# Measured matmul steps, concurrent row halves and one shared port in the model that orders a streaming trunk's matmuls

## The chip, the cores and the metric

The kernel runs on one NeuronCore of one Trainium2 chip. The metric is device time in microseconds of one execution; the median of several runs is compared. Time before: 3200.01 us median of 3 runs (3194.38 to 3201.84).

## The reference

One mixer layer over 2048 tokens of width 1024, all in float32. The input is normalised and modulated, projected by one matrix, and split over three branches (latent attention, a chunked gMLP, RWKV-7); each branch is gated, projected, weighted by a sigmoid gate and summed; the sum is projected again, normalised and added to the input.

```python
shift, scale, gate = jnp.split(c_act @ w_ada[l] + b_ada[l], 3, axis=-1)
h = rmsnorm(x, pre_g[l]) * (1 + scale[:, None]) + shift[:, None]
q_lat, kv_lat, k_rope, gm_in, rw_in, z, g_logit = split_last(h @ w_in[l], IN_SPLITS)
y_mla = mla_mixer(q_lat, kv_lat, k_rope, ...)      # block-causal softmax attention, 8 heads
y_gm = gmlp_mixer(gm_in, ...)                      # u * (W_s v + b) in blocks of 128
y_rw, v_first = rwkv7_mixer(rw_in, ...)            # delta-rule state, 8 heads of 64
branches = jnp.stack([y_mla, y_gm, y_rw], axis=2) * silu(z)
proj = jnp.einsum('bsnw,nwd->bsnd', branches, w_br[l])
merged = jnp.sum(proj * jax.nn.sigmoid(g_logit), axis=2)
y = merged @ w_out[l]
x = x + gate[:, None] * rmsnorm(y, post_g[l])
```

## The kernel before

The tokens go in four super-blocks of 512 (s = 0 to 3). For each, a stage `wkv(s)` computes RWKV-7 and a stage `attention(s)` the latent attention. The large projections (`gemm`) are split products: activations and weights are each a high and a low float32r part, and `mm3` makes three matmuls of 512 columns for every 128 rows (`hh`, `hl` are the activations' parts, `wh`, `wl` the weights', `brh`, `brl` a branch's parts, `pd` the PSUM tile). A `gemm` over the width of 1024 is 24 such matmuls, one over half of it 12. ScalarE makes `wh`, and GpSimd or VectorE, whichever has the shorter backlog in the model, makes `wl` (`split`). The small steps of RWKV-7 and the transposes are plain float32.

TensorE takes its instructions in the order in which the program is written, and that order is made by a planner, the class `Pace`. Every piece of work is a generator (a thread) that yields what its next matmuls need: tiles, or a free PSUM tile of a ring (`RD`, `RS`, `RT`, `RO`: two of `pd`, three of `pss`, two of `pst`, one of `pso`). `Pace.run` keeps a rough clock of all engines. Of the threads whose needs are met by that clock, the first in rank goes on: rank 0 and 1 are the stage's own chains, 3 the projections of the next super-block (`todo`), 4 the gates and merges that only fill (`later`). Where no chain is ready, a filler runs until one is. So the clock decides how many `gemm` matmuls stand between two steps of a chain.

`Pace.note` advances that clock. It gives every instruction a duration, and `Pace.slot` finds the first free time of its engine. A result counts for another engine `HOP` = 0.25 us after its end. Weights are placed up to `EAR` = 8 us early (`pace.early`), and `gemm` then forgets them (`pace.forget`), so that no thread waits for them in the model. The lines that the change meets:

```python
if eng == "PE":
    dur = n * (4 if f32 and not i.is_transpose else 2 if f32 else 1) / 2400
    t = self.t = max(self.t, dep) + dur
...
    dur = .05 + n * .00084 + .04 * (not psum) + ...      # ScalarE
...
t = self.slot(eng, max(dep, self.t - self.early), dur) + dur
```

The chains that are spoken of below, all in `wkv`, once for each head pair `hp` of 0 to 3. `prepare`: two products per PSUM tile (`pst<-ard,bk`), ScalarE copies `abc`, VectorE masks `ak` and `MB`, then `m_ak_v` (`pso<-vt,ak`); ahead of it `v` is transposed into a `pst` tile that VectorE must first have read for `kk`. `inverses`: 31 steps on `X` through `tx`, all on VectorE and all in SBUF. `advance`: `pss<-Pm,xtb`, `pss<-u,m`, `pss<-n,xtb`, `pss<-MB,Wm` (64 rows, in the upper and the lower half of the array by turns), `pss<-UV,MB`. `states`: eight times `pss<-S,QG` with VectorE between them, then a normalisation over VectorE, ScalarE and GpSimd, and the transposes `pss<-consts,Y`. From s = 1 on, the output rows of the super-block before are finished in the same stage (`back`: `pst<-consts,yo`). A helper records every operation, so all of them have line 121.

Of the kernel before, what the change touches and what calls it, by code (L numbers as in the profile page):

```python
# [21 lines left out]
P = 128  # L22
# [69 lines left out]
class Pace:  # L92
    """Order of the tensor engine's work. Threads are generators that yield what their next piece of it needs:
    tiles (the last write to them), names of rings (a free tile), conditions. A rough clock of all engines says
    when a need should be met; of the threads whose need is met, the first in rank goes on."""
# [3 lines left out]
    def __init__(self):  # L99
        self.t = 0.0  # L100
        self.early = 0.0
        self.wrote, self.used = {}, {}
        self.busy = {}
        self.rings = {}
        self.lock = None
        self.cur = None
        self.threads = []
        self.pe = 0.0
        self.spent = 0.0
        self.table = None  # L110
        self.slots = {}

# [18 lines left out]
    def slot(self, eng, t, dur):  # L131
        """first time from t on at which the engine is free for dur"""
        b = self.busy.setdefault(eng, [])
        while b and b[0][1] < self.t - 60:
            b.pop(0)
        for n, (s, e) in enumerate(b):
            if t + dur <= s:
                b.insert(n, (t, t + dur))
                return t
            t = max(t, e)  # L140
        b.append((t, t + dur))
        return t
# [5 lines left out]
    def note(self, i):  # L148
        eng = str(i.engine).split(".")[-1]
        dma = "DMA" in type(i).__name__  # L150
        src, dst, n, full, f32 = [], [], 1, 0, False
        for l, aps in ((src, i.ins), (dst, i.outs)):
            for a in aps:
# [10 lines left out]
                if eng != "PE" or l is dst:  # L164
                    n = max(n, m)
# [8 lines left out]
        if eng == "PE":  # L174
            dur = n * (4 if f32 and not i.is_transpose else 2 if f32 else 1) / 2400
            t = self.t = max(self.t, dep) + dur
            self.pe += dur
# [5 lines left out]
        else:  # L183
            psum = any(x.startswith(("pd", "ps")) for x in src)
            op = type(i).__name__
            if eng == "Activation":
# [4 lines left out]
                dur = .05 + n * .00084 + .04 * (not psum) + .09 * (len(src) > 1) + .09 * (len(dst) > 1)  # L191
# [11 lines left out]
            t = self.slot(eng, max(dep, self.t - self.early), dur) + dur  # L203
# [10 lines left out]
    def forget(self, *tiles):  # L214
        """no wait for the last write to them"""
# [3 lines left out]
    def pool(self, pl, bufs):  # L219
        """its tiles wait for the last use of the tile that had their place"""  # L220
# [48 lines left out]
    def run(self, until, share=0.0, spare=lambda: True):  # L269
        """until the condition holds; per time of the threads of rank 0 and 1, share of those of rank 3;  # L270
        while nothing is to spare, the threads of rank 4 run only where the others wait for long"""
# [33 lines left out]
def trunk(ctx, tc, io, out):  # L305
# [38 lines left out]
    # ---------------------------------------------------------------- constants  # L344
# [13 lines left out]
    def rstd_of(dst, src, mul, eps, n):  # L358
        """dst = (src * mul + eps) ** -0.5"""
# [24 lines left out]
    with ExitStack() as st:  # L384
# [3 lines left out]
        # c -> silu(c) as columns  # L388
# [29 lines left out]
        # halves of the biases that go inside tanh(x / 2), and of k_a  # L418
# [6 lines left out]
        # x of the first super-block, normalised and transposed  # L425
# [58 lines left out]
    def output_gate(pl):  # L484
        """gate of the modulation times post_g, for all partitions"""
# [21 lines left out]
    # ---------------------------------------------------------------- shared pieces  # L507
# [24 lines left out]
    def split(hi, lo, src, e=None):  # L532
        """hi + lo == src, both float32r"""
# [6 lines left out]
    def wgran(src):  # L540
        """a [512, 128] piece of a weight matrix: [128 rows, 4, 128] high and low"""
# [13 lines left out]
    def gemm(w, c0, rhs, nk=KD, r0=0):  # L555
        """features c0..c0+127 of rhs' tokens, features on the partitions"""
# [16 lines left out]
    def silu2(n, f):  # L573
        """2 * silu(z) of branch n, features f"""
# [7 lines left out]
    def br_split(b2, pl=brp):  # L582
        """half of b2 as high and low"""
# [9 lines left out]
    def front_units(s, pl):  # L593
        """normalised, modulated input of a super-block, transposed, as high and low"""
# [72 lines left out]
    # ---------------------------------------------------------------- latent attention: projections  # L667
# [14 lines left out]
    def trig_of(s, pl):  # L682
        """rows 64..95: cosine, rows 96..127: signed sine"""
# [18 lines left out]
    def rope(dst, src, trig, t1, t2):  # L702
        """src rows 64..95 hold the halves, rows 96..127 the halves exchanged"""
# [4 lines left out]
    def mla_units(s, pl):  # L708
# [28 lines left out]
        def norms():  # L737
            """1 / rms of every token as a column, then as a row for all partitions"""
# [98 lines left out]
    # ---------------------------------------------------------------- gMLP  # L837
# [42 lines left out]
    def gm_gates(s):  # L880
        """the spatial gates times gelu(u) and 2 * silu(z)"""
# [17 lines left out]
    # ---------------------------------------------------------------- RWKV-7  # L899
    def latents():  # L900
        """of the decay and of the rate"""
# [14 lines left out]
    def wkv(s):  # L916
# [6 lines left out]
        with ExitStack() as st:  # L923
# [32 lines left out]
            def prepare(hp, r, k, v, sq, kk):  # L956
                pc = slice(hp * P, (hp + 1) * P)
                # decay, cumulated inside the chunks
# [18 lines left out]
                # squared norm of kk  # L977
# [18 lines left out]
                # b = kk * a / |kk|^2 with a = (1 + ta) / 2  # L996
# [13 lines left out]
                # tokens on the partitions  # L1010
# [13 lines left out]
                # products between the tokens of a chunk  # L1024
# [54 lines left out]
                # bonus  # L1079
# [10 lines left out]
            def inverses(hp, mb):  # L1090
                """of the 32 x 32 diagonal blocks; partition 32 g + x has rows g, g + 4, ... of block x's"""
# [21 lines left out]
            def advance(hp, xd, ard, el, Pm, vt, MB, abc):  # L1113
# [11 lines left out]
                # diagonal of the chunks' decays  # L1125
# [5 lines left out]
                # U = (I - M)^-1 [A | M_ak V]  # L1131
# [46 lines left out]
                # what a chunk adds by itself: output and state  # L1178
# [10 lines left out]
            def states(hp, zs, bv, QG, YH):  # L1189
                """chunk by chunk, then the normalised output"""  # L1190
# [18 lines left out]
                # normalisation over a head's channels  # L1209
# [64 lines left out]
    # ---------------------------------------------------------------- latent attention  # L1274
# [436 lines left out]
```

## Time and profile before

| | |
|---|---|
| time, median of 3 runs | 3200.01 us (3194.38 to 3201.84) |
| span of the profiled execution | 3209.0 us |
| TensorE busy | 3008.7 us, 94% |
| VectorE busy | 1943.6 us, 61% |
| ScalarE busy | 1473.8 us, 46% |
| GpSimd busy | 1186.6 us, 37% |
| mean granted clock of TensorE | 0.965 |

Read it so: TensorE (PE) is busy nearly all of the span, and its busy time counts a matmul until its modelled end, which overlaps the next one. VectorE (DVE) is busy 61%, ScalarE (ACT) 46%, GpSimd (POOL) 37% of the span. The granted clock is 1 where TensorE runs at 2.4 GHz and 0.5 where it runs at 1.2 GHz. The profiled execution's span lies 9 us over the median of the runs, and its own time is not listed apart from it.

### The profile page before, as it was taken

The page shows a single profiled execution, that of the slowest core. Times are in us where ns is not written, and L with a number is a line of the kernel's source. Part 1 is how long each engine was busy: PE and PEld are TensorE (multiplying, and loading weights), DVE is VectorE, ACT ScalarE, POOL GpSimd, SP SyncE. Part 2 cuts the span into 40 slices and gives each one's busy share as a digit, 9 for nine tenths or more (in the row PEclk, how much of TensorE's full clock was granted, in tenths as well). Part 3 has the DMA queues.
Part 4 walks back from the last instruction along what each step waited for, and adds up shares of the span by engine and source line. Part 5 has one row for each costly group of instructions (what it writes and reads, how often), then busy time and mean ns, then how long its engine had stood idle before and what let it go on. Part 6 is the DMA issues. An engine that isn't in the chain of part 4 may idle for free.

```text
span 3209.0 us, 47580 instructions
## 1 busy us (share of the span) xinstructions
PE 3008.7 (94%) x15900; PEld 2472.8 (77%) x15900; DVE 1943.6 (61%) x4800; ACT 1473.8 (46%) x3234; POOL 1186.6 (37%) x1114
## 2 busy tenths in 40 slices
PE   5899999989999999999999998999899999999998
PEld 4687777778777777878878776887787777788876
DVE  7436674474477765566367674557736766667653
ACT  4343332544433336555433434565444334477743
POOL 3333333343523334244443334224334333433324
PEclk8999999989999999999999998999999999999999
DMA  7443333745542466444544366444345425643345
GB/s 252 117 128 99 81 82 89 208 131 145 152 139 83 133 190 179 135 132 121 158 136 116 113 179 188 112 126 131 95 136 146 125 82 167 189 110 103 90 127 168
DMA packets 594113, 432.70 MB, mean 135 GB/s; under 512 B 143216, under 2 KB 489420, under 8 KB 593868
## 3 DMA queue, kind: packets, MB, share of 16 engines
q1 hardware_dynamic: 593696, 429.62, 47.0%
q8 instruction: 125, 2.05, 0.3%
q14 instruction: 120, 0.98, 0.1%
q10 hardware_dynamic: 172, 0.05, 0.0%
HBM read 328.61 MB, written 100.93 MB: 134 GB/s over the span
## 4 chain that ended last, share of the span: by engine, by line
PE 61%; DVE 21%; DMA 5%; issue 4%; ACT 2%; POOL 2%; SPq 1%; DVEq 0%; POOLq 0%; ACTq 0%
PE pd L121 37%; PE pst L121 11%; PE pss L121 9%; PE pso L121 5%; DVE X L121 4%; DVE tx L121 4%; DMA x<-in_x 2%; DVE y L121 1%; DVE QG L121 1%; DVE Y L121 1%; SPq L121 1%; DMA stg<-q_d 1%; DVE wl L121 1%; DVE gt L121 1%; DVE k L121 1%
## 5 line engine op out<-in xcount | busy, mean ns | idle before, releaser
L121 POOL TENSOR_TENSOR wl<-wr,wh 128x512 fp32r<-128x512 f32 x498 | 657.3, 1321 | 1111.3 <-ACT wh L121 1069.9
L121 PE MATMUL pd<-hh,wh 128*128 128x512 f32 x1952 | 810.8, 415 | 5.5 <-ACT hh L121 2.5
L121 PE MATMUL pd<-hl,wh 128*128 128x512 f32 x1952 | 771.3, 395 | 3.7 <-POOL hl L121 2.6
L121 PE MATMUL pd<-hh,wl 128*128 128x512 f32 x1952 | 771.8, 395 | 1.9 <-POOL wl L121 1.2
L121 ACT ACTIVATE wh<-wr 128x512 fp32r<-128x512 f32 x648 | 406.8, 629 | 796.9 <-PE pd L121 431.4
L121 PEld LDWEIGHTS pd<-hh,wl 128*128 128x128 f32 x1952 | 370.7, 190 | 85.6 <-DVE wl L121 1.8
L121 PEld LDWEIGHTS pd<-hh,wh 128*128 128x128 f32 x1952 | 372.0, 191 | 82.4 <-ACT wh L121 6.8
L121 PEld LDWEIGHTS pd<-hl,wh 128*128 128x128 f32 x1952 | 372.6, 191 | 68.9 <-POOL hl L121 3.6
L121 DVE TENSOR_TENSOR pw<-pst,ph 128x512 fp32r<-128x512 f32 (+2 forms) x352 | 196.3, 567 | 200.3 <-ACT ph L121 198.9
L121 PE MATMUL pd<-brh,wh 128*128 128x512 f32 x576 | 260.7, 453 | 30.9 <-DVE X L121 12.9
L121 ACT ACTIVATE ph<-pst 128x512 fp32r<-128x512 f32 (+2 forms) x352 | 171.9, 496 | 187.1 <-PE pst L121 155.0
L121 PE MATMUL pd<-brl,wh 128*128 128x512 f32 x576 | 239.3, 416 | 1.8 <-DVE brl L121 1.8
L121 PE MATMUL pd<-brh,wl 128*128 128x512 f32 x576 | 239.3, 415 | 0.0
L121 ACT ACTIVATE p<-p,nm 128x512 f32<-128x512 f32 (+3 forms) x288 | 189.5, 660 | 62.9 <-DVE nm L121 62.7
L121 DVE TENSOR_SCALAR_CACHE_REDUCE p<-pss 128x512 f32<-128x512 f32 (+2 forms) x320 | 192.2, 606 | 29.4 <-PE pss L121 25.5
L121 DVE TENSOR_TENSOR wl<-wr,wh 128x512 fp32r<-128x512 f32 x150 | 119.9, 801 | 85.3 <-ACT wh L121 77.9
L121 PE MATMUL pst<-consts,p 128*128 128x128 f32 x1088 | 162.7, 274 | 9.3 <-DVE otm L121 4.5
L121 PEld LDWEIGHTS pd<-brh,wh 128*128 128x128 f32 x576 | 116.4, 202 | 69.3 <-issue 24.3
L121 PE MATMUL pso<-ph,v 128*128 128x256 f32 x576 | 154.0, 289 | 2.3 <-ACT ph L121 2.3
L121 PE MATMUL pso<-pw,v 128*128 128x256 f32 x576 | 148.2, 285 | 4.0 <-DVE pw L121 2.3
L121 PEld LDWEIGHTS pst<-consts,p 128*128 128x128 f32 x1088 | 128.9, 141 | 27.6 <-DVE otm L121 5.0
L121 DVE TENSOR_TENSOR tx<-X,mb 128x60 f32<-128x60 f32 (+19 forms) x368 | 140.0, 380 | 8.7
(297 smaller groups left out, 5363.4 us busy)
## 6 DMA issues: line engine op xcount, KB each, us to landing
wr<-in_w_in SPq DMA_DIRECT2D x480, 256.0 KB
wr<-in_w_br SPq DMA_DIRECT2D x96, 256.0 KB
gate_d<-gt SPq DMA_DIRECT2D x64, 256.0 KB
part_d<-gt SPq DMA_DIRECT2D x64, 256.0 KB
p<-part_d SPq DMA_DIRECT2D x64, 256.0 KB
wr<-in_w_out SPq DMA_DIRECT2D x64, 256.0 KB
x<-in_x SPq DMA_DIRECT2D x56, 256.0 KB
gt<-gate_d SPq DMA_DIRECT2D x56, 256.0 KB
```

Of the source, the lines that this page charges most:

```text
L121: r = f(*a, **k)
```

## The change

Only the model's numbers and rules change; no operation of the computation does.

- TensorE, float32r: n / 2400 + 0.0135, at least 0.061 us, for n columns (512 columns: 0.227 for 0.213).
- TensorE, float32: twice max(0.111, n / 1200) (64 columns: 0.222 for 0.107; 128 columns: 0.222 for 0.213; 1 or 2 columns: 0.222 for about 0.002). Float32 transposes at least 0.108.
- A matmul on other rows of the array than the ones that began with it starts with them in the model, and adds only what it ends later (`beside`).
- ScalarE: 0.08 for 0.05 as the fixed part.
- GpSimd's instructions, and those of VectorE that read no PSUM, also occupy a common "port" in the model, so that they stand after each other.

```diff
+        self.beside = 0.0, [(0, P)]
...
-    def slot(self, eng, t, dur):
-        """first time from t on at which the engine is free for dur"""
-        b = self.busy.setdefault(eng, [])
-        while b and b[0][1] < self.t - 60:
-            b.pop(0)
-        for n, (s, e) in enumerate(b):
-            if t + dur <= s:
-                b.insert(n, (t, t + dur))
-                return t
-            t = max(t, e)
-        b.append((t, t + dur))
+    def slot(self, eng, t, dur, also=()):
+
+        lists = [self.busy.setdefault(e, []) for e in (eng, *also)]
+        for b in lists:
+            while b and b[0][1] < self.t - 60:
+                b.pop(0)
+        moved = True
+        while moved:
+            moved = False
+            for b in lists:
+                for s, e in b:
+                    if t < e and s < t + dur:
+                        t, moved = e, True
+        for b in lists:
+            insort(b, (t, t + dur))
         return t
...
         if eng == "PE":
-            dur = n * (4 if f32 and not i.is_transpose else 2 if f32 else 1) / 2400
-            t = self.t = max(self.t, dep) + dur
-            self.pe += dur
+            if f32 and not i.is_transpose:
+                dur = 2 * max(.111, n * 2 / 2400)
+            elif f32:
+                dur = max(.108, n * 2 / 2400)
+            else:
+                dur = max(.061, n / 2400 + .0135)
+            (r, c), (nr, nc) = i.tile_position, i.tile_size
+            if dep <= self.t and all(r >= b or r + nr <= a for a, b in self.beside[1]):
+
+                at = self.beside[0]
+                self.beside[1].append((r, r + nr))
+            else:
+                at = max(self.t, dep)
+                self.beside = at, [(r, r + nr)]
+            t, p = max(self.t, at + dur), self.t
+            self.pe += t - max(p, at)
+            self.t = t
...
-                dur = .05 + n * .00084 + .04 * (not psum) + .09 * (len(src) > 1) + .09 * (len(dst) > 1)
+                dur = .08 + n * .00084 + .04 * (not psum) + .09 * (len(src) > 1) + .09 * (len(dst) > 1)
...
-            t = self.slot(eng, max(dep, self.t - self.early), dur) + dur
+
+            port = ("port",) if eng == "Pool" or eng == "DVE" and not psum else ()
+            t = self.slot(eng, max(dep, self.t - self.early), dur, port) + dur
```

Every engine's order moves nearly throughout, and the number of matmuls stays (14001). The pattern of `wkv` repeats for s = 1, 2 and 3, before and after; the three places here are of s = 3. In the change the recording helper stands on line 123.

The first place is TensorE's order in `prepare` of head pair 1, from the products `ard`, `bk` to the first use of the masked `ak`. Before:

```order
8457 L121 MATMUL pst<-ard,bk 128x128 x8
8458 L121 MATMUL pd<-hh,wh 128x512
8459 L121 MATMUL pd<-hl,wh 128x512
8460 L121 MATMUL pd<-hh,wl 128x512
8461 L121 MATMUL pd<-hh,wh 128x512
8462 L121 MATMUL pd<-hl,wh 128x512
8463 L121 MATMUL pd<-hh,wl 128x512
8464 L121 MATMUL pd<-hh,wh 128x512
8465 L121 MATMUL pd<-hl,wh 128x512
8466 L121 MATMUL pd<-hh,wl 128x512
8467 L121 MATMUL pso<-vt,ak 128x64 x2
8468 L121 MATMUL pst<-ard,bk 128x128 x4
```

And the same step in the change:

```order
8502 L123 MATMUL pst<-ard,bk 128x128 x8
8503 L123 MATMUL pd<-hh,wh 128x512
8504 L123 MATMUL pd<-hl,wh 128x512
8505 L123 MATMUL pd<-hh,wl 128x512
8506 L123 MATMUL pso<-vt,ak 128x64 x2
8507 L123 MATMUL pst<-ard,bk 128x128 x4
8508 L123 MATMUL pd<-hh,wh 128x512
8509 L123 MATMUL pd<-hl,wh 128x512
8510 L123 MATMUL pd<-hh,wl 128x512
8511 L123 MATMUL pso<-vt,ak 128x64 x2
```

Three `gemm` matmuls stand ahead of the first `ak` step where nine stood, and three more stand ahead of the second, where there was none.

The second place is VectorE's queue ahead of that same `ak`: the last ten rows of it, which are the end of `inverses` of head pair 0 (`X`, `tx`) and one eviction of the merge (`gt`). Before:

```order
3159 L121 TENSOR_TENSOR X<-X,tx 128x7x4
3160 L121 TENSOR_TENSOR tx<-X,mb 128x24
3161 L121 TENSOR_TENSOR X<-X,tx 128x8x3
3162 L121 TENSOR_TENSOR tx<-X,mb 128x16
3163 L121 TENSOR_TENSOR X<-X,tx 128x8x2
3164 L121 TENSOR_TENSOR tx<-X,mb 128x8
3165 L121 TENSOR_TENSOR X<-X,tx 128x8
3166 L121 SCALAR_TENSOR_TENSOR gt<-gt,pd 128x512
3167 L121 TENSOR_TENSOR gt<-gt,p_24818 128x512
3168 L121 TENSOR_TENSOR ak<-pst,consts 128x256
```

In the change, from the last `bk` of the head pair on:

```order
3216 L123 TENSOR_TENSOR bk<-kk,Ei 128x4x128
3217 L123 TENSOR_TENSOR X<-X,tx 128x7x5
3218 L123 TENSOR_TENSOR wl<-wr,wh 128x512
3219 L123 TENSOR_TENSOR tx<-X,mb 128x28
3220 L123 MEMSET sg 128x8
3221 L123 TENSOR_TENSOR X<-X,tx 128x7x4
3222 L123 TENSOR_TENSOR tx<-X,mb 128x24
3223 L123 TENSOR_TENSOR X<-X,tx 128x8x3
3224 L123 TENSOR_TENSOR tx<-X,mb 128x16
3225 L123 TENSOR_TENSOR X<-X,tx 128x8x2
3226 L123 TENSOR_TENSOR tx<-X,mb 128x8
3227 L123 TENSOR_TENSOR X<-X,tx 128x8
```

Rows 3228 to 3230 are then the two `gt` and the `ak` as before. Behind the last `bk` stand nine rows of `X` and `tx` and one `wl`. Before, the last `bk` is row 3153 and eleven such rows follow it: the end of the inverse still lies ahead of `ak`, with two rows fewer and a `wl` more.

The third place is TensorE's order in `advance` of head pair 1. Before:

```order
8564 L121 MATMUL pss<-MB,Wm 64x128 x16
8565 L121 MATMUL pss<-UV,MB 128x64 x8
8566 L121 MATMUL pd<-hh,wh 128x512
8567 L121 MATMUL pd<-hl,wh 128x512
8568 L121 MATMUL pd<-hh,wl 128x512
8569 L121 MATMUL pss<-UV,MB 128x64 x8
8570 L121 MATMUL pd<-hh,wh 128x512
8571 L121 MATMUL pd<-hl,wh 128x512
8572 L121 MATMUL pd<-hh,wl 128x512
8573 L121 MATMUL pss<-sst,QG 128x64 x2
```

And in the change:

```order
8607 L123 MATMUL pss<-UV,MB 128x64 x8
8608 L123 MATMUL pd<-hh,wh 128x512
8609 L123 MATMUL pd<-hl,wh 128x512
8610 L123 MATMUL pd<-hh,wl 128x512
8611 L123 MATMUL pd<-hh,wh 128x512
8612 L123 MATMUL pd<-hl,wh 128x512
8613 L123 MATMUL pd<-hh,wl 128x512
8614 L123 MATMUL pd<-hh,wh 128x512
8615 L123 MATMUL pd<-hl,wh 128x512
8616 L123 MATMUL pd<-hh,wl 128x512
8617 L123 MATMUL pss<-UV,MB 128x64 x8
8618 L123 MATMUL pss<-sst,QG 128x64 x2
```

Nine `gemm` matmuls stand between the two halves of `UV` where three stood.

## Rows read from the trace of the kernel before

**Rows 1.** The profile's page: span, busy time, granted clock in 40 slices.
```profile
span 3209.0 us, 47580 instructions
PE 3008.7 (94%) x15900; PEld 2472.8 (77%) x15900; DVE 1943.6 (61%) x4800; ACT 1473.8 (46%) x3234; POOL 1186.6 (37%) x1114
PEclk8999999989999999999999998999999999999999
```

**Rows 2.** Waits of TensorE: who, for whom, us in total, times, longest.
```profile
PE pso L121 <- DVE ak L121: 17.2, 6, 4.2
PE pd L121 <- DVE X L121: 12.9, 3, 4.3
PE pss L121 <- DVE Y L121: 9.1, 7, 2.2
PE pss L121 <- DVE p L121: 7.8, 4, 3.5
PE pst L121 <- DVE h L121: 7.5, 3, 4.7
...
PE pst L121 <- DVE kk L121: 4.8, 3, 1.7
...
PE pss L121 <- DVE S L121: 3.9, 10, 1.2
PE pst L121 <- DVE yo L121: 3.5, 6, 0.7
```

**Rows 3.** Timeline of TensorE at the first place: start, length, engine, operation, count, [idle].
```profile
2484.41 1.71 PE L121 MATMUL pst<-ard,bk 64*128 64x128 f32 x16
2486.05 0.50 PE L121 MATMUL pd<-hh,wh 128*128 128x512 f32 x1
2486.39 0.40 PE L121 MATMUL pd<-hl,wh 128*128 128x512 f32 x1
...
2488.00 0.39 PE L121 MATMUL pd<-hh,wl 128*128 128x512 f32 x1
2492.60 1.11 PE L121 MATMUL pso<-vt,ak 128*128 128x64 f32 x4 [4.22 <-DVE ak L121]
```

**Rows 4.** Timeline of all engines at that place: VectorE and GpSimd.
```profile
2487.06 1.30 POOL L121 TENSOR_TENSOR wl<-wr,wh 128x512 fp32r<-128x512 f32 x1
...
2487.18 1.21 DVE L121 TENSOR_TENSOR tx<-X,mb 128x28 f32<-128x28 f32 x1
...
2488.43 0.19 DVE L121 TENSOR_TENSOR X<-X,tx 128x28 f32<-128x28 f32 x1
```

**Rows 5.** Windows around that wait: busy us by engine, then granted clock, DMA.
```profile
2485.00:2492.00 7.00, 3.39 (x23) 2.54 (x21) 6.66 (x12) 1.72 (x5) 4.62 (x4) 1.00 0.26 76
2492.00:2503.00 11.00, 10.40 (x40) 9.14 (x41) 3.74 (x10) 1.68 (x5) 0.37 (x1) 0.53 0.54 133
```

**Rows 6.** Timeline of TensorE at the third place.
```profile
2527.90 1.96 PE L121 MATMUL pss<-MB,Wm 64*64 64x128 f32 x32
2529.79 2.00 PE L121 MATMUL pss<-UV,MB 128*128 128x64 f32 x16
2531.60 0.48 PE L121 MATMUL pd<-hh,wh 128*128 128x512 f32 x1
...
2533.68 2.00 PE L121 MATMUL pss<-UV,MB 128*128 128x64 f32 x16 [1.14 <-ACT YH L121]
```

**Rows 7.** Timeline at the end of `states`, head pair 1, s = 3.
```profile
2615.76 2.96 POOL L121 TENSOR_TENSOR wl<-wr,wh 128x512 fp32r<-128x512 f32 x2
2615.82 1.77 DVE L121 TENSOR_TENSOR Y<-Y,rs 128x512 f32<-128x512 f32 x1 [1.65 <-POOL rs L121]
...
2617.74 0.63 PE L121 MATMUL pss<-consts,Y 128*128 128x128 f32 x4 [1.25 <-DVE Y L121]
```

**Rows 8.** The instructions on tile `wl`: count, duration ns min/median/max.
```profile
L121 POOL TENSOR_TENSOR wl<-wr,wh x498: 1256/1291/1922, 34.9 to 3187.9; 128x512 fp32r<-128x512 f32 x166
L121 DVE TENSOR_TENSOR wl<-wr,wh x150: 665/692/3054, 178.7 to 3115.7; 128x512 fp32r<-128x512 f32 x150
```

More of the change, by code (lines that the diff above doesn't have):

```diff
@@ L1 @@
 import math
+from bisect import insort
 from collections import deque
```

## The prediction

> **What bounds the kernel now.** I read the page first. TensorE is busy 94% of 3209.0 us, VectorE 61%, ScalarE 46%, GpSimd 37% [rows 1]. So the order of TensorE's own stream sets the end, and what an order can change is the time in which that stream waits, and the stretches at the lower clock that follow. Next I read the waits of TensorE. No single one is large, and those that lead the list are released by VectorE: `ak` 17.2 us in 6 waits, `X` 12.9 in 3, `Y` 9.1 in 7, `p` 7.8, `h` 7.5, `kk` 4.8, `S` 3.9, `yo` 3.5 [rows 2]. The eight together are 66.7 us, 2% of the span: this is the stock that a better order can draw on, and that a worse one adds to.
>
> Then I read the timeline at the longest of them. After the products `ard`, `bk`, nine `gemm` matmuls run, and then TensorE stands for 4.22 us until `ak` is there [rows 3]. VectorE is not idle in that time: it is busy 6.66 of 7.00 us [rows 5], with the small steps of an inverse. The step `tx` of 28 elements takes 1.21 us where GpSimd's `wl` (1.30 us) began just before it, and the next step, of the same size, takes 0.19 us without one [rows 4]. So VectorE waits for GpSimd in such steps, and `ak` stands behind them in VectorE's queue. After the wait the granted clock is 0.53 for 11 us, where it was 1.00 [rows 5]: at half speed, that costs about 5 us more.
>
> **The model's new numbers against the trace.** A float32r matmul starts every 0.23 us (2486.39 to 2488.00, seven steps) [rows 3]; the model had 0.213 and now has 0.227. Eight float32 products of 64 columns take 1.81 us (2529.79 to 2531.60, two records each), 0.226 us each, where it had 0.107 and now has 0.222 [rows 6]. The sixteen of `MB`, `Wm` take 1.89 us, 0.118 each, since upper and lower halves run side by side; it had 0.213 each and now charges a pair 0.222 [rows 6]. So TensorE's numbers become right. But TensorE's clock in the model was too fast, by 6% in the fillers and by half in small products, and that was a margin: other engines seemed later, counted in matmuls, than they are, and more filler was put between the steps of a chain. The change takes this margin away. Against it work 0.03 us more on each ScalarE instruction and the port.
>
> The Trainium skill (SBUF — State Buffer, section on the two separate sides) says that GpSimd and VectorE share one port pair as an exclusive lock for a whole instruction, when the VectorE instruction has two SBUF inputs. The 1.21 against 0.19 us of [rows 4] agrees, though GpSimd's own `wl` keeps a median of 1291 ns [rows 8]. By that page the port term of the model is right in kind, which speaks for the faster rival below.
>
> **Part by part.** Fill between two steps is counted from the order, in matmuls at 0.23 us. A wait that had a row gets longer by what it loses.
>
> 1. *End of `states`.* Between the last `S` and the transposes of `Y` there stand, for s = 1 to 3 alike, 33 and 39 `gemm` matmuls in head pairs 0 and 1, now 27 and 33; head pair 3 keeps 33; head pair 2 loses about 1.9 us of mixed work. Head pair 1 waits 1.25 us already, behind a `Y` of 1.77 us that met GpSimd's `wl` [rows 7], so it pays 6 x 0.23 = 1.4 us in each of three stages: 4.2. Head pair 0 showed no large wait, so its chain needs at most some 7.6 us and it pays between 0 and 1.4; I take 1.4, since 27 matmuls are 6.2 us and head pair 1's chain took 39 x 0.23 + 1.25 = 10.2. Sum +8; bounds +4 (head pair 1 alone) and +14 (head pair 2 too).
>
> 2. *`ak`.* In head pair 1, six matmuls fewer are 1.4 us, and in VectorE's queue two steps of `X` fewer and a `wl` more stand ahead of `ak`. The steps are worth 0.19 to 1.21 each [rows 4], the `wl` 0.69 [rows 8]: from -1.7 to +0.3, I take -0.8. So +0.6 in each of three stages, +2. In s = 0 two `ak` lose nine matmuls each (2.1 us) and one gains 4.2 us of fill, which can take away no more than the 3.1 us or so that is left of the 17.2 [rows 2]: +1. Of the 128 `ak` steps, 33 now have under 1.5 us of fill, where 9 had. Their price has no row of its own. The nearest is `S`, whose steps have as little fill: 3.9 us in 10 waits, of 224 steps [rows 2]; that is 0.02 to 0.4 us, I take 0.1 for each of the 24: +2. Sum +5; bounds -4 and +15.
>
> 3. *`yo`.* In each of three stages one of these transposes goes from 14 matmuls of fill to 8, one from 14 to 11, and one gains two: 1.4 + 0.7 - 0.4 = 1.7, and these are the ones with waits (3.5 us in 6, and others put down to `X`) [rows 2]. Sum +5; bounds 0 and +6.
>
> 4. *`v` behind `kk`.* The three waits of 4.8 us [rows 2] are head pair 0's, and its fill stays. Head pairs 1 and 3 go from 23 to 11 and from 14 to 8 matmuls. Head pair 0's chain needed 1.8 us of fill and 1.6 of wait, 3.4; by that they pay at most 0.9 and 1.6. Sum +3; bounds 0 and +7.
>
> 5. *`UV` and `S`.* Six more matmuls (1.4 us) between the halves of `UV` in head pair 1 take away the 1.14 us of [rows 6], three times: -3. In head pair 3 the same step loses three matmuls and one step of `S` in head pair 1 does too: 0 to 0.7 each, six times, I take +3. Sum 0; bounds -3 and +4.
>
> 6. *Changes of form.* The first `gemm` matmul after a float32 one takes 0.34 us to the next (2486.05 to 2486.39) and not 0.23 [rows 3]. There are 700 such changes for 722: 22 x 0.11 = -2.
>
> 7. *Attention.* Its waits do not repeat from stage to stage. Of those for `p` and `h` (7.8 and 7.5 us) [rows 2] five get between 1.4 and 5.1 us more fill: up to -10 if none opens elsewhere. I take -8; bounds -10 and +10, since the same reshuffle takes fill from hand-offs that had just enough.
>
> 8. *GpSimd to VectorE.* 15 of the 498 `wl` go from GpSimd (1.29 us) to VectorE (0.69) [rows 8]: 10 us more on an engine that is busy 61%, 19 less on the one it waits for. I count 0; what hides it is VectorE's idle time, and where the chain of `X` has none, each costs up to 0.69 us: +10 at most.
>
> Sum: 8 + 5 + 5 + 3 + 0 - 2 - 8 = +11 us, 0.3%. The profiled span of 3209.0 would be 3220. It lies 9.0 us over the median of the runs, 3200.0, and the same step on that median gives 3211. I count no further cost of the clock: a wait of 4.22 us was followed by a fall [rows 5], and the forecast lengthens short waits by about 1 us and leaves that one.
>
> **The rivals.** *The port pays.* The model now knows why VectorE is late, and lays enough filler at the right places. For it: the longest waits stand exactly where VectorE's small steps meet GpSimd [rows 3, 4], and head pair 2's `ak` steps now have 4.4 to 10.7 us of fill where they had 2.7 to 4.9. Against it: at the longest wait the end of the inverse still stands ahead of `ak`, with less filler. If half of the 66.7 us goes, and with half of the long ones (`ak`, `X`, 30 us) as much again in clock [rows 2, 5], it is 33 + 15 = 48 us less; if a third goes, 22 + 10 = 32. The middle of the two is 3160. It decides from the point at which `ak` and `X` lose more than the 21 us that terms 1 to 4 add. *Short fills cost clock too.* Terms 1 to 5 at their upper bounds are 46, attention returns nothing, 2 come back from term 6: +44 before any clock: 3244. For it: the chains of `Y` and `ak` are late by VectorE's queue, which a shorter fill meets sooner; against it: most of these hand-offs showed no wait before, so the bounds add up unknown slack. *Nothing to see.* Waits move and their sum stays: 3200.
>
> **How the numbers follow.** What a measurement of this kernel can tell from no change is about 0.2%, 6.4 us. Forecast (own range 3196 to 3228): 0.42, of which 0.04 falls under 3194, 0.12 within, 0.26 over 3206. The port pays: 0.31, faster. Short fills cost clock: 0.14, slower. Nothing to see: 0.13, of which 0.02 faster, 0.09 same, 0.02 slower. Together faster 0.37, same 0.21, slower 0.42. The range for 8 in 10 reaches from 3148 to 3244: below it lies about a third of the port's case, above it half of the short fills'.
>
> **What would show it.** Right: the transposes of `Y` wait more than 9.1 us in all, `yo` more than 3.5, `ak` at least its 17.2, the wait between the halves of `UV` is gone, and the waits for `p` and `h` fall below 15. The port's case would show as waits for `ak` and `X` of under 15 us together and a granted clock without the 0.53 stretch. The forecast is wrong if `Y` and `ak` fall in spite of the shorter fill: then VectorE's queue, not the fill, is what moved. It is also wrong if the sum of waits stays and the time moves: then steps, clock or weights did it.

## The result

The changed kernel takes 3291.06 us (3284.59 to 3297.88) where the kernel before takes 3200.93 on the same chip: ratio 1.0281, 95% interval 1.0258 to 1.0303, 90 us slower. The forecast was 3211, and its range ended at 3244. The profiled execution took 3284.59 us with a span of 3282.8.

The page of the changed kernel, the same lines as [rows 1]:

```profile
span 3282.8 us, 47564 instructions
PE 3031.5 (92%) x15900; PEld 2489.7 (76%) x15900; DVE 1942.1 (59%) x4825; ACT 1478.2 (45%) x3236; POOL 1161.2 (35%) x1089
PEclk8999999999998989999999989999999989999999
```

No engine has more work: VectorE is busy 1942.1 us for 1943.6, GpSimd 25 us less. TensorE's busy time grows by 22.8 us with the same 15900 matmuls: some of them ran slower. TensorE's idle time grows by 51.0 us (251.3 for 200.3). Together that is 73.8 us, the difference between the two profiled spans; the medians differ by 90. The mean granted clock is 0.956, in the kernel before 0.965. The lower of its two levels is half of the upper (0.50 in the windows below), so the shares of the span at the lower level are 2 x 0.044 and 2 x 0.035: 289 us now, 225 before. At half speed these 64 us more cost about 32, if TensorE is busy in all of them.

The rest is in the waits of TensorE. Of the changed kernel (total, times, longest):

```profile
PE pd L123 <- DVE gt L123: 22.5, 9, 3.8
PE pst L123 <- DVE kk L123: 16.8, 9, 3.6
PE pst L123 <- DVE X L123: 15.3, 3, 5.7
PE pss L123 <- DVE p L123: 15.1, 6, 6.7
PE pss L123 <- DVE S L123: 14.2, 10, 2.1
...
PE pst L123 <- ACT sq L123: 11.3, 6, 3.8
PE pd L123 <- DVE lastp L123: 10.8, 8, 1.9
PE pd L123 <- DVE tx L123: 9.4, 3, 3.1
PE pd L123 <- DVE wl L123: 7.7, 1, 7.7
PE pss L123 <- DVE Y L123: 6.9, 10, 1.1
...
PE pss L123 <- ACT YH L123: 6.2, 9, 0.7
...
PE pst L123 <- DVE tx L123: 2.6, 3, 0.9
...
PE pst L123 <- DVE h L123: 2.1, 1, 2.1
...
PE pso L123 <- DVE ak L123: 0.5, 1, 0.5
```

And six lines of the kernel before that the rows ahead of the prediction left out:

```profile
PE pd L121 <- DVE gt L121: 6.8, 6, 2.8
...
PE pst L121 <- ACT sq L121: 6.0, 4, 3.9
PE pd L121 <- DVE lastp L121: 5.6, 5, 1.5
...
PE pss L121 <- ACT YH L121: 2.7, 3, 1.1
...
PE pst L121 <- DVE tx L121: 2.3, 3, 0.8
PE pst L121 <- DVE X L121: 2.3, 3, 0.8
```

Read against [rows 2], `ak` has all but gone (17.2 to 0.5) and `Y` has fallen (9.1 to 6.9), while `gt`, `kk`, `S` and `p` have risen by 15.7, 12.0, 10.3 and 7.3 us. The waits of `pst` put down to `X` and `tx` are transposes of `yo` in both kernels (`yo` stands behind these steps in VectorE's queue): with `yo`'s own line they were 8.1 us and are 17.9. An inconspicuous line, `YH` with nine waits of 0.69 us, turns out to be worth more than five times its 6.2 us.

### The profile page after: what moved, and what is told of

Its sections match the earlier page's. It is cut to its first block, busy times and chain, and to the rows that moved or that the text cites. A ratio compares the mean times of both kernels' runs of the same rounds, so it can differ in the third digit from the quotient of the medians.

```text
span 3282.8 us, 47564 instructions
## 1 busy us (share of the span) xinstructions
PE 3031.5 (92%) x15900; PEld 2489.7 (76%) x15900; DVE 1942.1 (59%) x4825; ACT 1478.2 (45%) x3236; POOL 1161.2 (35%) x1089
## 5 line engine op out<-in xcount | busy, mean ns | idle before, releaser
L123 POOL TENSOR_TENSOR wl<-wr,wh 128x512 fp32r<-128x512 f32 x483 | 634.6, 1315 | 1145.3 <-ACT wh L123 1094.5
L123 DVE TENSOR_TENSOR wl<-wr,wh 128x512 fp32r<-128x512 f32 x165 | 138.9, 843 | 86.1 <-ACT wh L123 82.3
L123 PE MATMUL pss<-kh,qh 96*128 96x512 f32 (+2 forms) x320 | 131.0, 409 | 17.2 <-DVE p L123 15.1
```

The lines of the kernel that those rows point to most:

```text
L123: r = f(*a, **k)
```

## The nine waits of 0.69 us

TensorE in `advance` of head pair 1 in s = 1, the kernel before (start, length, operation, count):

```profile
1011.16 1.96 PE L121 MATMUL pss<-MB,Wm 64*64 64x128 f32 x32
1013.05 3.79 PE L121 MATMUL pss<-UV,MB 128*128 128x64 f32 x32
1016.68 0.61 PE L121 MATMUL pso<-vt,ak 128*128 128x64 f32 x4
```

The same place in the changed kernel, up to the third step of `states`:

```profile
1008.41 1.96 PE L123 MATMUL pss<-MB,Wm 64*64 64x128 f32 x32
1010.30 2.00 PE L123 MATMUL pss<-UV,MB 128*128 128x64 f32 x16
1012.99 2.96 PE L123 MATMUL pss<-UV,MB 128*128 128x64 f32 x16 [0.69 <-ACT YH L123]
1015.88 1.11 PE L123 MATMUL pss<-sst,QG 64*128 64x64 f32 x4
...
1027.43 0.66 PE L123 MATMUL pss<-S,QG 64*128 64x64 f32 x4
```

In both, the two halves of `UV` stand directly behind each other, with no `gemm` matmul between them. But in the changed kernel the second half waits until ScalarE has copied the first half out (`YH`): both halves were given the same PSUM bank. Which of the three banks of the pool a `pss` tile gets is decided by the framework while it lays out the program; it isn't in the order of instructions. Three of the sixteen `UV` products have a shared bank in the kernel before, nine in the changed one. Windows around the one above and two others (length, busy time by engine, granted clock, DMA):

```profile
1008.00:1013.80 5.80, 5.11 (x60) 4.68 (x59) 5.28 (x20) 1.14 (x3) 0.00 (x0) 1.00 0.01 3
1013.80:1027.40 13.60, 13.60 (x57) 11.88 (x56) 2.40 (x9) 4.17 (x10) 4.09 (x4) 0.50 0.20 50
...
1103.90:1109.40 5.50, 4.81 (x40) 4.51 (x39) 3.74 (x17) 1.19 (x2) 0.74 (x2) 1.00 0.17 51
1109.40:1112.80 3.40, 3.40 (x11) 2.36 (x10) 2.96 (x7) 1.47 (x8) 1.81 (x2) 0.50 0.26 80
1173.00:1177.60 4.60, 3.91 (x35) 3.71 (x33) 4.34 (x16) 0.60 (x1) 0.00 (x0) 1.00 0.63 192
1177.60:1194.60 17.00, 17.00 (x45) 12.09 (x44) 5.43 (x14) 2.75 (x5) 2.54 (x2) 0.50 0.37 121
```

TensorE stands for 0.69 us, and within 3 us of the wait's end the clock goes from 2.4 to 1.2 GHz for 3.4 to 17 us in which TensorE is busy throughout. That happens at all nine places; the nine stretches are together 85.3 us. In the kernel before no fall follows any of the three waits for `YH`; there three `gemm` matmuls stand between the halves.

## The experiments

Three things could explain 90 us: the new numbers put too little filler everywhere (then each part of the change costs its share), the shared banks and the clock, or merely that the order is another one. An order that the planner makes of one set of numbers is called a draw below, since a small change of a number gives another. The first four runs split the change and try a meaningless edit.

**e1_steps**: the kernel before with TensorE's new steps alone.

```diff
-            dur = n * (4 if f32 and not i.is_transpose else 2 if f32 else 1) / 2400
...
+            if f32 and not i.is_transpose:
+                dur = 2 * max(.111, n * 2 / 2400)
+            elif f32:
+                dur = max(.108, n * 2 / 2400)
+            else:
+                dur = max(.061, n / 2400 + .0135)
```

> The kernel before with the new steps of TensorE alone (float32r and float32), without concurrent halves, port or ScalarE's 0.03. Theory margin (TensorE's clock in the model was too fast, and this spare fill held the chains): the loss is here, 3260 to 3310 us. Rival port (the shared port delays VectorE's results in the model and moves fill to wrong places): 3190 to 3215. Rival reshuffle (any new order loses, since the waits fall elsewhere by chance): anything from 3200 to 3300, and the 1% jitter run moves as far.

Measured: 3339.62 us, ratio 1.0441 (1.0375 to 1.0507), clock 0.948.

**e2_port**: the kernel before with the shared port in `slot` alone.

> The kernel before with the shared port alone. Theory margin: the port makes VectorE's results later in the model, so more fill stands between steps: 3150 to 3210. Rival port: the loss is here, 3260 to 3310. Rival reshuffle: 3200 to 3300.

Measured: 3241.81 us, ratio 1.0126 (1.0092 to 1.0159).

**e3_jitter**: the kernel before with an edit without meaning, in the float32r step alone.

```diff
-                dur = n / 2400
+                dur = n / 2376
```

> The kernel before with a float32r matmul at n / 2376 for n / 2400 in the model, 1% more, which has no meaning but moves the order of some 2800 rows of TensorE. Theories margin and port: 3190 to 3225, at most a sixth of the loss. Rival reshuffle: 3230 or more, or a gain of the same size.

Measured: 3232.63 us, ratio 1.0090 (1.0063 to 1.0118).

**e4_margin**: the changed kernel with the lost margin given back to the other engines.

```diff
-HOP = 0.25
-SLOW = 1.0
+HOP = 0.266
+SLOW = 1.065
```

> The changed kernel with the durations of the other engines times 1.065 in the model and a hop of 0.266 for 0.25 us, so that their ratio to a float32r matmul is again that of before. Theory margin: most of the loss comes back, 3180 to 3230 us. Rival port: the loss stays, 3260 to 3310. Rival reshuffle: any value, and the waits move to other places.

Measured: 3264.01 us, ratio 1.0193 (1.0165 to 1.0222), clock 0.951. The steps alone lose more than the whole change, and more than the margin theory allowed for; the port alone loses 1.3%, and one per cent on a number, which means nothing, 0.9%, both within the range of the reshuffle alone. e4 gets back some 28 us, not most of the loss as the margin theory expected. So the parts don't add up, and a part's ratio holds the cost of a new order too.

The next two take the banks by themselves. **e5_rotate_after** hands the banks out by turns; TensorE's order stays, row for row, that of the changed kernel. **e6_rotate_before** does the same to the kernel before.

```diff
-    ps_s = pool("ps_s", PSS, PSUM)
+    ps_s = [pool(f"ps_s{i}", 1, PSUM) for i in range(PSS)]
+    ns = [0]
...
-        return pace.ring("s", ps_s.tile([P, 512], F32, tag="s", name="pss"))
+        ns[0] += 1
+        return pace.ring("s", ps_s[ns[0] % PSS].tile([P, 512], F32, tag="s", name="pss"))
```

> The changed kernel with one edit: the three PSUM banks of the tiles pss are handed out strictly by turns; TensorE's order stays row for row that of the changed kernel. In its trace nine of the sixteen UV products have the second half in the very bank that the first half has just filled, so TensorE stands 0.69 us for ScalarE's YH there (nine waits, 6.2 us), and at all nine places the granted clock falls behind it, for 85.5 us in sum. Theory one (the shared bank makes the wait and the wait lets the clock fall): the nine waits go, the stretches at the lower clock at those nine places go, about 6 + 85.5 / 2 = 49 us come back: 3242, ratio to the kernel before about 1.013, mean clock from 0.956 to about 0.968. Rival (the clock falls because the 64-column products now run with no gemm matmul between them, wait or not): the waits go, the low stretches stay, 3285, ratio 1.026. Second rival (the bank by turns moves waits to VectorE's QG, which has the other half's bank): new waits for QG of 1 us and more at these places, 3285 or longer.

> The kernel before with the same edit alone: pss banks strictly by turns, TensorE's order row for row as before. Three UV products have the shared bank there (0.93 to 1.14 us each) and one of them a fall of the clock of 10.2 us. Theory one: 3.2 + 5 = 8 us less, 3193, ratio 0.9975 (0.995 to 1.000). Rival (the framework's own choice of bank was good elsewhere, turns cost waits behind VectorE's slower evictions): ratio 1.002 or more, with waits for QG, u1 or S that the kernel before doesn't have.

Measured: e5 3259.22 us, ratio 1.0174 (1.0141 to 1.0208), clock 0.964; e6 3215.84 us, ratio 1.0043 (1.0026 to 1.0060). The place shown above, in the timeline of e5:

```profile
1007.75 1.96 PE L123 MATMUL pss<-MB,Wm 64*64 64x128 f32 x32
1009.64 3.79 PE L123 MATMUL pss<-UV,MB 128*128 128x64 f32 x32
1013.36 0.65 PE L123 MATMUL pss<-sst,QG 64*128 64x64 f32 x4
```

The window of e5 from `MB`, `Wm` to that same step of `S`:

```profile
1007.75:1019.71 11.96, 11.96 (x111) 10.78 (x110) 7.28 (x27) 5.02 (x13) 3.34 (x4) 1.00 0.11 31
```

The changed kernel needs 19.03 us for the same matmuls (1008.41 to 1027.43), e5 11.96: a wait of 0.69 us cost 7.1. Over the whole kernel it is 1.07% of 3201, 34 us, and not the 49 expected, because by turns the second half has the bank of the first half of `MB`, `Wm`, and at head pair 3 VectorE is still adding `QG` from it (timeline of e5, s = 1):

```profile
1164.20 2.00 PE L123 MATMUL pss<-UV,MB 128*128 128x64 f32 x16
1167.39 1.97 PE L123 MATMUL pss<-UV,MB 128*128 128x64 f32 x16 [1.19 <-DVE QG L123]
```

There the clock falls again: 27 us at the lower level at the three such places, of the 85.3. In e6 these waits are long (12.3 us in 5, up to 3.7), and there was little to win: the expectation put the kernel before's fall of 10.2 us behind a shared bank, but it follows a wait of 0.93 us for `QG`, and the three waits for `YH` (0.71, 0.83 and 1.14 us) have no fall behind them. The Trainium skill (Perfetto Trace Analysis, section Optimizing Tensor Performance) advises to rotate independent groups through different PSUM banks. e5 agrees by 34 us; e6 doesn't, 14 us longer: at its five waits for `QG` VectorE was still reading the bank whose turn it was.

**e7_small_steps** and **e8_gemm_step** split e1: the kernel before with the float32 steps alone, and with the float32r step alone.

> The kernel before with the new steps of the float32 matmuls alone (0.222 us for 64 columns in place of 0.107, transposes at least 0.108); float32r stays at n / 2400, no port, no row groups, no ScalarE offset. Theory A (the gemm matmuls' 6% were the margin, small products matter little): ratio 1.00 to 1.01, what a reshuffle alone gave (1.009). Theory B (the doubled price of the small products is what takes fill out of the chains of S, UV and ak): ratio 1.02 or more. Four UV products have the shared bank in this order.

> The kernel before with the new step of the float32r matmuls alone (n / 2400 + 0.0135, 0.227 us for 512 columns in place of 0.213). Theory A (this margin of 6% is what the chains lived on): ratio 1.02 or more, waits at short fills spread over S, ak, p and gt. Theory B (a reshuffle like any other): 1.00 to 1.01. Three UV products have the shared bank in this order, as before.

Measured: e7 3268.56 us, ratio 1.0204 (1.0165 to 1.0244); e8 3241.11 us, ratio 1.0118 (1.0087 to 1.0149). Taken alone the small products' price costs more, as theory B of e7 had it, and the 6% on `gemm` about what a reshuffle does. Each is one draw, and e10 below does not bear the first out.

**e9_reshuffle_down**: the kernel before with `dur = n / 2424`, the other meaningless direction. **e10_without_small_steps**: the changed kernel without the float32 steps. **e11_rotate_and_margin**: e4 and e5 together. **e12_fill_before**: the kernel before, and ahead of each half of `UV`

```diff
+FILL = 1.4
...
+                    t0 = pace.t + FILL
+                    yield (lambda: pace.t >= t0,)
                     yield (RS, UV, MB)
```

> The kernel before with float32r steps 1% too short (n / 2424) where the run e3_jitter had them 1% too long: a second change of the model without meaning. Theory R (the order of before is a good draw, and any other draw costs about as much as e3's 0.9%): ratio 1.005 to 1.015. Rival (e3 was slow because its steps went in the same direction as the change, towards longer gemm steps; shorter ones add filler and help): 0.995 to 1.002. Four UV products have the shared bank.

> The changed kernel without the new steps of float32 matmuls (they keep n x 4 / 2400 and n x 2 / 2400), all the rest of the change in it: gemm step, row groups, ScalarE's 0.03, the port. Theory one (the doubled price of the small products is the largest single part, e7 1.0204 alone): ratio 1.005 to 1.015, like a reshuffle; kk and gt waits fall by half. Rival (the parts cost what they cost whatever else is there, gemm step 1.2% and port 1.3%): 1.02 to 1.03. Five UV products have the shared bank, where the changed kernel has nine.

> The changed kernel with the banks of pss by turns, as in e5, and the margin of e4 (every duration of the other engines times 1.065, the hop 0.266 us). e4's order has two shared banks in place of nine, so its gain of 27 us may have been the bank's alone. Theory M (what is left after e5 is fill that is too short, and the margin gives it back): ratio 1.005 to 1.012, sum of the waits for kk, gt, S and lastp well under e5's 61 us. Theory N (e4 gained by the bank, the margin itself does little): 1.015 to 1.02, the same as e4 and e5.

> The kernel before with one rule more: 1.4 us of other work by the model's clock ahead of each half of the UV product. No half shares a bank then, and no half runs directly behind the other. Hope: the three waits for YH (2.7 us) and the fall of 10.2 us go, nothing else opens: 3192 to 3200, ratio 0.996 to 0.999. Theory R (any other draw of the order costs about 0.9%): 1.005 to 1.015, with new waits in places that have nothing to do with UV.

Measured: e9 3240.08 us, ratio 1.0135 (1.0085 to 1.0185). e10 3264.23 us, 1.0197 (1.0170 to 1.0225): my theory of it fell; it came out next to the rival's range, though e8 and e2 together give 2.4%. e11 3248.77 us, 1.0161 (1.0133 to 1.0188): the same as e5 within the intervals, so the margin did little there once the banks were separate (theory N), and what e4 won may have been the bank's. e12 3249.45 us, 1.0156 (1.0133 to 1.0180): no `UV` product waits for `YH` any more (one waits 0.3 us for `QG`), the hope of 3192 to 3200 fell, and waits open in places that have nothing to do with it:

```profile
PE pss L124 <- ACT kh L124: 27.8, 4, 9.8
PE pso L124 <- DVE ak L124: 22.5, 8, 3.8
PE pss L124 <- DVE Y L124: 14.1, 11, 2.2
PE pss L124 <- DVE S L124: 14.0, 10, 3.1
```

By then every edit of the kernel before had cost 0.4 to 4.4%, meant or not. The last six ask how draws of the new model stand against draws of the old, and test the bank once more. **e13_after_up** and **e14_after_down**: the changed kernel with n / 2376 and n / 2424. **e15_before_hop** and **e18_before_hop_down**: the kernel before with HOP 0.255 and 0.245. **e16_after_down_rotate** and **e17_before_hop_rotate**: e14 and e15 with the banks by turns.

> The changed kernel with the float32r step n / 2376 + 0.0135 (about 1% up), an edit without meaning. Three UV products share a bank, where the changed kernel has nine. Theory D (most of the change's 2.8% is the draw of the order plus the shared banks): ratio 1.012 to 1.02. Rival (the new model itself puts too little fill everywhere): 1.024 to 1.032, as the changed kernel.

> The changed kernel with the float32r step n / 2424 + 0.0135 (about 1% down). Ten UV products share a bank. Theory D: 1.022 to 1.032, about what nine shared banks cost in the changed kernel, with a fall of the granted clock behind most of the ten. Rival (the bank is not what counts): 1.012 to 1.02.

> The kernel before with HOP 0.255 in place of 0.25, an edit without meaning. Seven UV products share a bank, where the kernel before has three. Theory D: a draw (0.9 to 1.4%) and four more shared banks (0.3 to 0.5%): 1.012 to 1.02. Rival (small edits of the old model mostly change nothing, e3 and e9 were misfortune): 0.998 to 1.005.

> e14 with the pss banks by turns, TensorE's order row for row that of e14: ten shared banks to none. Theory one: the ten waits for YH and the falls behind them go, 20 to 40 us less than e14 (ratio to the kernel before lower by 0.007 to 0.012), of which some comes back as waits for QG. Rival (e5's gain was a reshuffle on VectorE): within 0.4% of e14.

> e15's TensorE order, row for row, with the pss banks by turns: seven shared banks to none. In e15 the waits for YH (six us in seven) have no fall behind them. Theory C (the bank costs through the clock, and only where a fall follows): the gain is at most the waits, 5 us, and new waits for QG take it back as in e6: ratio 0.995 to 1.002. Rival (a shared bank costs 3 to 5 us each whatever follows, as e14 against e16 seems to say): 25 us less than e15, ratio 0.989.

> The kernel before with HOP 0.245 in place of 0.25, an edit without meaning; three shared banks, as before. Theory R (draws of the old model scatter between 0.997 and 1.014, the kernel before at the good end): 1.003 to 1.014. Rival (HOP within 2% hardly matters, e15): 0.996 to 1.002.

Measured: e13 3252.63 us, 1.0143 (1.0100 to 1.0187); e14 3281.81 us, 1.0239 (1.0194 to 1.0284); e15 3195.80 us, 0.9968 (0.9946 to 0.9990); e16 3235.78 us, 1.0107 (1.0070 to 1.0144); e17 3217.26 us, 1.0053 (1.0030 to 1.0075); e18 3223.93 us, 1.0066 (1.0050 to 1.0083). e9, e13, e14 and e18 lie within the ranges of their theories, e16 gained slightly more than its theory gave; e15 and e17 lie outside both of the ranges that they were given.

e14 against e16 repeats e5: the same TensorE order, ten shared banks to none, 1.32% or 42 us. The mean clock goes from 0.954 to 0.965. In e14 the clock falls behind nine of the ten. e15 is the contrary case, and the only version that beats both kernels. It has seven shared banks with a wait at each. In three of them `gemm` matmuls stand between the halves, as in the kernel before; in the other four the halves are back to back and wait the same 0.69 us, here at head pair 3 of s = 1 (timeline of e15):

```profile
1169.39 1.96 PE L123 MATMUL pss<-MB,Wm 64*64 64x128 f32 x32
1171.29 2.00 PE L123 MATMUL pss<-UV,MB 128*128 128x64 f32 x16
1173.97 2.00 PE L123 MATMUL pss<-UV,MB 128*128 128x64 f32 x16 [0.69 <-ACT YH L123]
1175.78 0.48 PE L123 MATMUL pd<-hh,wh 128*128 128x512 f32 x1
```

The windows of e15 up to the end of that product and behind it:

```profile
1169.40:1175.80 6.40, 5.71 (x66) 5.40 (x65) 6.22 (x20) 1.63 (x3) 1.57 (x1) 1.00 0.54 168
1175.80:1182.00 6.20, 6.20 (x31) 4.44 (x30) 2.00 (x6) 1.23 (x2) 1.29 (x1) 1.00 0.47 153
```

No fall follows, at none of the seven, and there giving each half its own bank doesn't help: e17 is 0.85% longer than e15, with 14.9 us of waits for `QG` in 8, six of them with a fall behind (1.5 in 2, one with a fall, in e15), and a clock of 0.965 for 0.970. Its loss of 27 us lies outside theory C's range, because the turns opened more waits and falls than they closed; the rival, 25 us to win, is far off. What theory C says of the cost, that a wait is dear where a fall of the clock follows, fits e5, e14 with e16, and e15; e17 doesn't test it by itself.

## Why the prediction was wrong

*What bounds the kernel* was right: the work of the engines didn't change, the order did. The direction was right; some 80 of the 90 us were not in the sum.

*"I count no further cost of the clock"* is the single step that failed most. The sentence took the 4.22 us of [rows 5] for what a fall needs, and held that short waits leave the clock alone. The runs show falls behind waits of 0.69 us. The added 64 us at the lower level are about 32 us. With the nine waits themselves the shared banks are worth 34 us in this order (e5).

*Term 5, `UV` and `S`, 0,* is mis-sized, and the place of its -3 was misread. It looked at the block of [rows 6], which is called head pair 1 ahead of the prediction but is the first `UV` product of its stage, head pair 0; that block got its nine matmuls, and its wait of 1.14 did go. In head pairs 1 and 2 nothing stands between the halves, before or now, and in head pair 3 the three matmuls went that the term priced at 0 to 0.7 us; so the order showed little. In those three head pairs of s = 1 to 3 the nine waits opened: `YH` went from 2.7 to 6.2 us. `S` cost +10.3, not the 0 to 4 that I gave it.

*Term 4, `v` behind `kk`, +3 (at most 7):* 4.8 to 16.8, +12.0, nine waits where there were three. Head pair 0's three stayed as they were, as the term said. Head pair 3 now waits 2.2 to 2.3 us in each of three stages (6.7 together), where the term, from head pair 0's chain, gave it at most 1.6; head pair 1, at most 0.9 there, doesn't wait. The other 5.3 us are three waits of s = 0, which it left out. *Term 3, `yo`, +5 (at most 6):* 8.1 to 17.9, +9.8. One transpose in each stage, the last of the eight, goes from 0.7 us to 4.0 to 5.7, where the term gave no single one more than 1.4: its `yo` stands behind the end of an inverse in VectorE's queue.

*Term 2, `ak`, +5:* 17.2 to 0.5. *Term 1, `Y`, +8:* 9.1 to 6.9. Both have the wrong sign; the order put less filler behind the step that these chains start from, and they waited less. By the prediction's own test, "then VectorE's queue, not the fill, is what moved". For `ak` the trace shows how. The place of [rows 3] in the changed kernel, TensorE and VectorE:

```profile
2554.02 1.71 PE L123 MATMUL pst<-ard,bk 64*128 64x128 f32 x16
2555.80 0.42 DVE L123 TENSOR_TENSOR ak<-pst,consts 128x256 f32<-128x256 f32 x1 [0.74 <-ACT abc L123]
2556.46 0.55 PE L123 MATMUL pso<-vt,ak 128*128 128x64 f32 x4
```

The six matmuls that are missing behind `ard`, `bk` now stand ahead of them: between the transposes of `v` and these products there are twelve where there were six. In that time VectorE finished the inverse, so that it even waited 0.74 us for ScalarE ahead of `ak`, which started 1.8 us behind the beginning of the products; before, it started 7.7 us behind it (2484.41 to 2492.13). Term 2 counted the fill between the two steps and the rows in VectorE's queue, but not the fill that had moved ahead of the first step and gave VectorE time to work that queue off.

*Term 7, attention, -8:* `p` and `h` went from 15.3 to 17.2. The reshuffle that was to close five waits opened as many elsewhere, which was its upper bound's argument. `gt`, `sq` and `lastp`, +26 us together, had no term at all.

*Term 8* was right in that GpSimd's work fell; its `wl` takes as long as before (1315 ns on average for 1321).

*The rivals.* "Short fills cost clock too" was the nearest, with 3244 and a chance of 0.14. "The port pays" had it half right, `ak` fell from 17.2 to 0.5, and still the time rose; the port alone costs 1.3% (e2).

**How the 90 us divide.** The banks are worth 34 us in the changed kernel (about 13 either way, by the two intervals), and 42 (19 either way) in another order, e14 and e16. TensorE's order is the same, row for row, in each pair; the framework, which orders the other engines itself, moved some 450 and 420 of VectorE's 4800 rows with it, so a part of either gain can be that. By the mean clock (0.964 for 0.956) e5 spends 54 us less at the lower level, about 27 of its 34 us. For the other 56 us there are only draws. The four meaningless edits of the kernel before (e15, e18, e3, e9) have a mean of (0.9968 + 1.0066 + 1.0090 + 1.0135) / 4 = 1.0065. The three orders of the new model in which the halves of `UV` don't wait for `YH` (e5, e16, e13) have (1.0174 + 1.0107 + 1.0143) / 3 = 1.0141. By that, about 0.65% (21 us) is that the kernel before was a good draw of its own model and most others lose it, 0.75% (24 us) what the new numbers cost on average, and 11 us how far e5 lies over its mean. With the banks by turns on both sides the middle part is larger: e6 and e17 have a mean of 1.0048, e5 and e16 of 1.0141, 0.9% apart. With a scatter of 0.7% between draws none of these parts is settled. That right numbers make a worse order than wrong ones is thus shown for the draws measured, not for the model as such.

**What stays open:** why the clock falls behind a wait of 0.69 us in the changed kernel and e14, eighteen times of nineteen, and in e15 at none of seven. A part of it shows in the twenty traces: where `gemm` matmuls stand between the halves, a wait for `YH` has a fall behind it once in 11, and 25 times in 33 where none does. The kernel before's three and three of e15's seven are of the first kind. The other four of e15 are of the second, and what TensorE runs right before them is nearly the same as in e14. And which part of the change costs the 0.75%: the parts don't add (e7 and e8 give 3.2%, together in e1 4.4; without the larger of them, e10, 2.0).

## What to carry to other kernels

When a planner's numbers change, the new order is a new draw. Before explaining the difference, time two or three meaningless edits of the same size: here they cost -0.3 to +1.4%, more than any term of the sum, and one of them, HOP 0.255, was worth 10 us.

Look at what the order doesn't show: which buffer or bank a tile gets. A short wait that repeats at the same place in a dense run of small matmuls is to be read with the granted clock behind it; the list of waits gave it 6.2 us, and taking it away gained 34. Separate the tiles only where the trace shows the fall, since the bank by turns cost 14 and 27 us in two other orders.

## What the runs showed of the hardware

Of 320 `UV` products in the twenty traces (sixteen each), 206 run without a wait of over 0.25 us inside; behind two of them the clock falls, counted from the start of the block to 3 us behind its end (four others begin at the lower level). Of the 44 whose second half waits for `YH` 26 have a fall behind them, of the 70 with a wait for `QG` 38. So such a block, 32 float32 matmuls of 64 columns, nearly always kept its clock where nothing interrupted it, even with no `gemm` matmul for 6 us and more (e5, 1007.75 to 1014), and behind one with an interruption a fall followed more often than not (64 of 114). The 0.25 us is where the count draws its line, nothing that was measured. That the wait brings the fall, and doesn't only go with it, rests on the two pairs of the same order. The Trainium skill (TensorE: Matmul & The Clock Gate, section A second HAM failure mode) tells of a bf16 kernel in which cycling through PSUM banks makes short idle times between groups of matmuls, often enough for the clock to swing; the rows here agree in that short idle times have falls behind them, and add that a single one of 0.69 us can have one in a stream that is otherwise full.
